# First tap of the gated recurrence's convolution on ScalarE; the WKV recurrence with its inverse's products unit by unit, a third buffer, and two output stores a half step

## The chip, the cores and the metric

The kernel runs on one core of one Trainium2 chip. The metric is device time in microseconds (us); the time before is the median of three runs. TensorE (PE), VectorE (DVE), ScalarE (ACT), GpSimd (POOL) and the queues that issue DMA transfers (here nearly all on SyncE, SP) run side by side, each in its own order. TensorE has two clocks, 1.2 and 2.4 GHz; the profile gives the granted share of the higher one.

## The reference, cut to what matters

One layer: a normed, modulated input `h` (1024 latent tokens and 256 context tokens, 1024 channels) goes through two token mixers, the merged result through a SwiGLU. The two recurrences:

```python
def directional_conv(u, w, bias, reverse):          # 4 taps per channel
    ...
    out = bias
    for j in range(LRU_CONV):
        off = LRU_CONV - 1 - j if reverse else j
        out = out + w[j] * up[:, off:off + L]
    return out
def wkv7_scan(r, w, k, v, a, b, S0):                # S: 16 heads of 64x64, two directions
    def step(S, inp):
        r_t, w_t, k_t, v_t, a_t, b_t = inp
        sa = jnp.einsum('dbhij,dbhj->dbhi', S, a_t)
        S = S * w_t[..., None, :] + sa[..., :, None] * b_t[..., None, :] + v_t[..., :, None] * k_t[..., None, :]
        y = jnp.einsum('dbhij,dbhj->dbhi', S, r_t)
        return S, y
```

The first recurrence (1280 channels, both directions) takes its gates from the convolved input and is a scan `h = a*h + b`. The second (WKV) is a matrix-valued scan over the tokens. After it, `y` of both directions is summed and group-normed per head.

## The kernel before

Float32 throughout; the dense products are split into a high and a low part and made in three matmuls (L88 to L90). By the trace the program has five stages: 95 to 760 us the in-projections with the first recurrence beside them; 760 to 1490 the operands of the WKV recurrence; 1490 to 2206 the WKV recurrence, with the last of its operands and of the 32x32 inverses beside its first steps, the output projection of the first recurrence (`pol`, L1107) and the group norms as fill; then the rest of the group norms and the merge; from 2345 the SwiGLU, in which TensorE is full. A scheduler puts each engine's instructions into an order from dependencies and priorities, so an edit in one place can move instructions of others.

**First recurrence** (`lru_tiles`). For each pair of 120-channel tiles, direction and stretch of tokens (512 wide, or 256 for the context), `conv` loads `lup` (L383), zeroes its edges on POOL (L380, L382), and makes `lxc` on VectorE: the first tap as a `tensor_scalar` with weight and bias (L386), three more taps on top (L388). Then `lh` and `ll` (L398, L399) feed the gate matmuls `pg` (L415), ScalarE makes the sigmoids and exponentials (L54), POOL two products (L430, L432), VectorE the scan. There are 66 tiles; `lxc` has four buffers and `lup` five. Each tile of the in-projection needs `whi` (VectorE, L230), `wlo` (POOL, L231), and an eviction of its result `pin` on ScalarE (L258, L296 and others).

**WKV recurrence** (`wkv_chain`). 32 tokens are one step; 40 steps, the first 8 the context's. The 16 heads of two directions are 32 units; each step has two half steps `a` = 0 and 1 of 16 units, in two chains that are woven together. The state and the step's other vectors sit in a tile `tvu` of 128 rows: 64 of state, 32 of `v` (loaded by L969 through `new_tvu`, one step ahead), 32 of `u`. A half step:

1. `ru`: 16 matmuls of 128 rows x 32 columns (out<-in `ru<-tvu,skb`), one a unit, four column groups in turn; copy to `rs` (helper L993, by turn on VectorE or ScalarE).
2. `rs` times the unit's inverse (`ru<-rs,xbd`): four matmuls of 128x128, each with a block-diagonal `xbd` of four 32x32 inverses. `xbd` is put together by four copies a step on VectorE (L1025, for both halves at once) from the loaded tile `xc`; POOL zeroed the rest once. Four copies (L993) take the result into `tvu[96:128]`.
3. `pn`: 16 matmuls of 128 rows x 64 columns make the next state, two copies (L993), or every second step products with the decay (L1063), put it into the other buffer of `tvu`.
4. `py`: 16 matmuls make the outputs (steps from 8 on), one copy to `ys`, and four stores (L1013) of 32x256 into `y_d[2, SEQ, D]`.

Group norms (L1246 to L1289) load 128 tokens of `v`, gate and both directions of `y`, one DMA each; six of the eight run within the recurrence.

The product with the inverses:

```python
for v in range(0 if UT else 4):
    mm(t[:, 1, v], xb[:, a * 4 + v].rearrange("p a b -> p (a b)"), r[:, v])
```

`t` (`ru`) is one PSUM bank of 2 KB a partition. `pm` (L676, an operand of the recurrence) is the only product now that uses tiles of fewer than 128 rows in its main stage: four 64x64 tiles in turn, and the two row halves write different banks.

Of the kernel before, what the change touches and what calls it, by code (L numbers as in the profile page):

```python
# [10 lines left out]
AF = mybir.ActivationFunctionType  # L11
ALU = mybir.AluOpType
# [17 lines left out]
NSTEP = T // 32  # L30
# [313 lines left out]
def lru_tiles(k, pool, ps):  # L344
# [6 lines left out]
    nc, act = k.nc, k.act  # L351
# [18 lines left out]
    def conv(p, d, q):  # L370
        o, w = LQ[q]
        base, end = (SEQ, T) if q == 0 else (0, SEQ)
        out = []
        for t in ts(p):
            r = slice(0, rows(t))
            up = tile_(f"lup{t}_{d}_{q}", "lup", (LT, 516))
            lo = o - 3 if d == 0 else o
            x, y = max(lo, base), min(lo + w + 3, end)
            if x > lo:
                nc.gpsimd.memset(up[r, 0:3], 0.0)  # L380
            if y < lo + w + 3:
                nc.gpsimd.memset(up[r, w:w + 3], 0.0)  # L382
            nc.sync.dma_start(up[r, x - lo:y - lo], k.ux_d[t * LT:t * LT + rows(t), x:y])  # L383
            xc = tile_(f"lxc{t}_{d}_{q}", "lxc")[r, 0:w]
            tap = lambda j: up[r, j:j + w] if d == 0 else up[r, 3 - j:3 - j + w]
            nc.vector.tensor_scalar(xc, tap(3), k.lcw[r, t, d, 3:4], k.lcb[r, t, d:d + 1], ALU.mult, ALU.add)  # L386
            for j in range(3):
                nc.vector.scalar_tensor_tensor(xc, tap(j), k.lcw[r, t, d, j:j + 1], xc, ALU.mult, ALU.add)  # L388
            out.append(xc)
        return out  # L390
# [69 lines left out]
    units = [(p, d, q) for p in range((NT + 1) // 2) for d in range(2) for q in LORD[d]]  # L460
    k.act_last = prev = None
    nxt = conv(*units[0])
    gws = None
    for n, u in enumerate(units):
        p, d, q = u
# [4 lines left out]
        cur = gates(*u, xcs, gws)  # L470
# [437 lines left out]
FILLA = 0  # L908
ROUNDS = ((0, 1), (2, 3), (4, 5), (6, 7), (8,), (9,))
FPTS = ((0, 0), (38, 1), (40, 1))  # L910
UT = 0
NEND = 3
SETV = 0
SETDVE = 0
XDVE = 40
XACT = 0
PACE = 1
MORE = (1, 2, 3)
NRD = 3
# [10 lines left out]
def wkv_setup(k):  # L930
    nc, bp = k.nc, k.bp
    z = lambda n, sh: bp.tile(sh, F32, name=n)
    k.ska = [z(f"ska{i}", [P, NU, 64]) for i in range(NRING)]
    k.skb = [z(f"skb{i}", [P, NU, 64]) for i in range(NRING)]
    for i, t in enumerate(k.ska):
        nc.scalar.copy(t[0:64], bcast(k.ident[0:64, 0:64], 1, NU))
    if not UT:
        k.xbd = [z(f"xbd{i}", [P, 8, 4, 32]) for i in range(2)]
        for t in k.xbd:
            (nc.vector if SETDVE & 2 else nc.gpsimd).memset(t, 0.0)  # L940
    k.tvu = [[z(f"tvu{a}_{i}", [P, 2, 8, 64]) for i in range(2)] for a in range(2)]
# [18 lines left out]
def chunk_id(s, d):  # L960
    b, c = chunk(s, d)
    return 4 * b + c


def new_tvu(k, s, a):
    nc = k.nc
    src = pair(k.v_d.rearrange("(c s) f -> c s f", s=32), chunk_id(s, 0), chunk_id(s, 1))
    t = k.tvu[a][s % 2]
    nc.sync.dma_start(t[64:96].rearrange("p d h i -> p d (h i)"), src[:, :, a * 512:a * 512 + 512].rearrange("d s f -> s d f"))  # L969
    return t  # L970

# [13 lines left out]
def wkv_chain(k, a):  # L985
# [3 lines left out]
    def mm(*a, **b):  # L989
        k.pe_last = nc.tensor.matmul(*a, **b, start=True, stop=True).ins.name  # L990
# [8 lines left out]
    def outputs(s, tvu):  # L999
        if s < 8:  # L1000
            return
        skb = k.skb[s % NRING]
        py = k.psb2.tile([P, 4, 64], F32, name=f"py{s}_{a}", tag="py", bufs=1)
        for v, g, gr, d, i in units:
            mm(py[gr, v], skb[:, unit(d, i), 0:32], tvu[:, d, i])
        ys = k.op.tile([P, 256], F32, name=f"ys{s}_{a}", tag="ys", bufs=4)
        copy(ys, py.rearrange("p v i -> p (v i)"))
        for d in range(2):
            r = 32 * chunk_id(s, d)
            for h in range(2):  # L1010
                g = 2 * d + h
                c = a * 512 + h * 256
                nc.sync.dma_start(k.y_d[d, r:r + 32, c:c + 256], ys[32 * g:32 * g + 32])  # L1013

    cur, nxt, prev = None, new_tvu(k, 0, a), None
    for t in k.tvu[a]:
        (nc.vector if a < SETV else nc.gpsimd).memset(t[96:P], 0.0)
    for s in range(NSTEP):
        ska, skb = k.ska[s % NRING], k.skb[s % NRING]
        if not UT:  # L1020
            xb = k.xbd[s % 2]
        if a == 0 and not UT:
            for g in range(4):
                gr = slice(32 * g, 32 * g + 32)
                (nc.scalar.copy if s < XACT else nc.vector.tensor_copy if s < XDVE else nc.gpsimd.tensor_copy)(xb[gr, :, g], k.xc[s // 4][gr, s % 4].rearrange("p a v t -> p (a v) t"))  # L1025
        prev, tvu = cur, nxt
        cur = tvu
        ahead = lambda: new_tvu(k, s + 1, a) if s + 1 < NSTEP else None
        if a == 1:
            nxt = ahead()  # L1030
        t = ps.tile([P, 2, 4, 64], F32, name=f"ru{s}_{a}", tag="ru", bufs=2)
        seen = slice(0 if s else 64, P)
        for v, g, gr, d, i in units:
# [4 lines left out]
        if a == 0:  # L1038
            if s > 0:
                outputs(s - 1, prev)  # L1040
            nxt = ahead()
            yield
        for v, g, gr, d, i in units if UT else ():
            mm(t[gr, 1, v], k.xc[s // 4][gr, s % 4, a, v], r[gr, v])
        for v in range(0 if UT else 4):
            mm(t[:, 1, v], xb[:, a * 4 + v].rearrange("p a b -> p (a b)"), r[:, v])
        for g in range(4):
            copy(tvu[96:P, g // 2, g % 2 * 4:g % 2 * 4 + 4], t[32 * g:32 * g + 32, 1])
        yield
# [184 lines left out]
def group_norm(k, pool, ps, tb, out=None):  # L1234
# [7 lines left out]
    flat = lambda t: t.rearrange("p a i -> p (a i)")  # L1242
    y, v, g = big("gy"), big("gv"), big("gg")
    y1 = k.c1p.tile([P, NH, 64], F32, name="gy1_7") if tb == 7 else big("gy1")
    for t, src in ((v, k.v_d), (g, k.gate_d), (y, k.y_d[0]), (y1, k.y_d[1])):
        nc.sync.dma_start(flat(t), src[tok])  # L1246
        for _ in range(GNY):
            yield
    yield
# [251 lines left out]
def scratch(k):  # L1501
    d = k.dpool
    t = lambda n, s: d.tile(s, F32, name=n)
    k.ux_d = t("ux_d", [LRU, T])
    k.lru_d = t("lru_d", [LRU, SEQ])
    k.uy_d = t("uy_d", [LRU, SEQ])
    k.gl_d = t("gl_d", [D, SEQ])
    k.gr_d = t("gr_d", [D, SEQ])
    k.gate_d = t("gate_d", [SEQ, D])
    k.rw_d = t("rw_d", [2, 2, P, KD, 512])  # L1510
    k.v_d = t("v_d", [T, D])
    k.skb_d = [t(f"skb{i}_d", [n, P, NU, 64]) for i, n in enumerate((NSTEP - 8, 8))]
# [183 lines left out]
```

## Time and profile before

| | |
|---|---|
| median of three runs | 3172.0 us (3169.22 to 3175.68) |
| profiled execution | 3170.86 us |
| its span | 3168.8 us |
| PE, DVE, ACT, POOL busy | 87%, 63%, 45%, 33% |
| mean granted PE clock | 0.904 |

The profile is one execution. Its page gives each engine's busy time, the span in 40 slices, the chain that ended last, and groups of instructions with the idle time ahead of them and what ended it; the trace behind it can be asked by stage, line, tile and stretch. "PEld" is the loading of weights into TensorE. A float32 matmul stands twice in the trace, so 16 matmuls are 32 records.

### The profile page before, as it was taken

How to read it: one execution, taken by the hardware profiler on the slowest of the kernel's cores; microseconds unless marked ns; L12 is line 12 of the kernel's file. 1: busy time of each engine (PE TensorE's matmuls, PEld its weight loads, DVE VectorE, ACT ScalarE, POOL GpSimd, SP SyncE). 2: the span in 40 equal slices, each digit the busy share in tenths (PEclk: the TensorE clock that was granted, in tenths of full speed). 3: DMA queues.
4: the chain of work that ended last, by engine and by line, in shares of the span. 5: the costliest groups of instructions: out<-in, count | busy, mean ns of one | idle time of the engine just before them, and what ended most of it. 6: DMA issues, size and time to landing. Idle time of an engine off the chain costs nothing. (4 is left out here: it accounts for less than half of the span.)

```text
span 3168.8 us, 53672 instructions
## 1 busy us (share of the span) xinstructions
PE 2772.7 (87%) x20606; PEld 2235.2 (71%) x20606; DVE 2010.8 (63%) x3067; ACT 1410.4 (45%) x2579; POOL 1037.3 (33%) x896
## 2 busy tenths in 40 slices
PE   5888888789898878887889878788899999999998
PEld 4767666667777666765666767566678888888888
DVE  7688989894667887878874434675686423232234
ACT  3465757474467555767333433344425111111114
POOL 4344435452445545666333220323441000000000
PEclk9999899999899878987558978788999999999999
DMA  5334333322455455555766777776772211111112
GB/s 201 105 107 128 115 109 118 111 76 74 142 145 143 114 123 128 131 140 136 192 189 213 220 210 206 222 240 220 266 284 85 98 57 54 37 57 40 46 57 71
DMA packets 374726, 428.96 MB, mean 135 GB/s; under 512 B 135446, under 2 KB 279238, under 8 KB 366534
## 3 DMA queue, kind: packets, MB, share of 16 engines
q1 hardware_dynamic: 374470, 425.53, 45.4%
q8 instruction: 163, 2.67, 0.4%
q14 instruction: 93, 0.76, 0.1%
HBM read 286.87 MB, written 126.26 MB: 130 GB/s over the span
## 5 line engine op out<-in xcount | busy, mean ns | idle before, releaser
L88 PE MATMUL pin<-h1024hi,whi 128*128 128x512 f32 (+1 forms) x1024 | 431.9, 422 | 47.0 <-DVE whi L230 15.2
L90 PE MATMUL pin<-h1024hi,wlo 128*128 128x512 f32 (+1 forms) x1024 | 425.8, 420 | 26.0 <-POOL wlo L231 16.8
L89 PE MATMUL pin<-h1024lo,whi 128*128 128x512 f32 (+1 forms) x1024 | 427.2, 417 | 4.1 <-DVE h1024lo L120 4.1
L231 POOL TENSOR_TENSOR wlo<-wraw,whi 128x512 fp32r<-128x512 f32 (+1 forms) x144 | 229.7, 1595 | 339.8 <-DVE whi L230 135.0
L88 PEld LDWEIGHTS pin<-h1024hi,whi 128*128 128x128 f32 (+1 forms) x1024 | 205.2, 201 | 100.8 <-DVE whi L230 21.3
L90 PEld LDWEIGHTS pin<-h1024hi,wlo 128*128 128x128 f32 (+1 forms) x1024 | 204.8, 200 | 80.6 <-POOL wlo L231 23.1
L89 PEld LDWEIGHTS pin<-h1024lo,whi 128*128 128x128 f32 (+1 forms) x1024 | 204.2, 199 | 51.3 <-DVE h1024lo L120 6.6
L54 ACT ACT_TABLE_LOAD x164 | 210.4, 1283 | 17.2 <-DVE gd L499 5.9
L990 PE MATMUL pn<-tvu,ska 128*64 128x64 f32 (+1 forms) x2496 | 159.8, 255 | 34.9 <-DVE tvu L993 20.1
L1444 DVE TENSOR_TENSOR sil<-sil,pfu 128x512 f32<-128x512 f32 x44 | 30.2, 687 | 243.2 <-PE pfu L90 243.2
L990 PEld LDWEIGHTS pn<-tvu,ska 128*64 128x64 f32 (+1 forms) x2496 | 122.8, 161 | 75.9 <-DVE tvu L993 23.3
L388 DVE SCALAR_TENSOR_TENSOR lxc<-lup,c_lru_conv_w,lxc 120x512 f32<-120x512 f32 (+3 forms) x198 | 159.4, 835 | 0.4
L1452 DVE SCALAR_TENSOR_TENSOR x<-pfo,modv,x 128x512 f32<-128x512 f32 (+1 forms) x112 | 74.2, 670 | 132.4 <-PE pfo L90 132.4
L990 PE MATMUL ru<-tvu,skb 128*32 128x64 f32 (+1 forms) x2560 | 107.7, 260 | 49.9 <-ACT tvu L993 26.0
L993 ACT COPY tvu<-ru 32x256 f32<-32x256 f32 x193 | 69.9, 362 | 151.8 <-DVE tvu L993 99.4
L68 ACT CAST whi_fi<-wraw_fi 128x1024 fp32r<-128x1024 f32 x48 | 50.6, 1053 | 168.3 <-PE pfg L89 53.0
L990 PE MATMUL ru<-rs,xbd 128*128 128x64 f32 x640 | 113.3, 335 | 12.4 <-ACT rs L993 8.3
L415 PE MATMUL pg<-lh,gw 120*120 120x512 f32 (+3 forms) x264 | 95.4, 373 | 32.4 <-DVE lh L398 29.7
L990 PEld LDWEIGHTS ru<-tvu,skb 128*32 128x32 f32 (+1 forms) x2560 | 69.5, 131 | 75.9 <-ACT tvu L993 28.5
L680 ACT COPY bc<-pm 32x256 f32<-32x256 f32 x160 | 98.5, 616 | 52.6 <-PE pm L676 50.3
L721 DVE TENSOR_TENSOR X<-X,it 128x62 f32<-128x62 f32 (+25 forms) x186 | 119.1, 640 | 3.9
L720 DVE TENSOR_TENSOR it<-bp,X 128x62 f32<-128x62 f32 (+25 forms) x186 | 118.3, 636 | 3.8
(374 smaller groups left out, 7660.8 us busy)
## 6 DMA issues: line engine op xcount, KB each, us to landing
skb<-skb_d SPq DMA_DIRECT2D x40, 1024.0 KB
wraw<-in_w_in_dram SPq DMA_DIRECT2D x142, 256.0 KB
wraw_fi<-in_w_ffn_in_dram SPq DMA_DIRECT2D x48, 512.0 KB
skb_d<-kr SPq DMA_DIRECT2D x160, 128.0 KB
ska_d<-km SPq DMA_DIRECT2D x160, 128.0 KB
skb_d<-km SPq DMA_DIRECT2D x160, 128.0 KB
ska<-ska_d SPq DMA_DIRECT2D x40, 512.0 KB
wmr<-in_w_modT_dram SPq DMA_DIRECT2D x32, 512.0 KB
```

Source lines behind the costliest of these rows:

```text
L54: ins = self.nc.scalar.activation(*a, **b).ins
L88: nc.tensor.matmul(out, wh, xh, start=first, stop=False)
L89: nc.tensor.matmul(out, wh, xl, start=False, stop=False)
L90: nc.tensor.matmul(out, wl, xh, start=False, stop=last)
L231: (nc.gpsimd if INLO else nc.vector).tensor_tensor(lo, raw, hi.bitcast(F32), ALU.subtract)
L388: nc.vector.scalar_tensor_tensor(xc, tap(j), k.lcw[r, t, d, j:j + 1], xc, ALU.mult, ALU.add)
L415: nc.tensor.matmul(pg[r, g, 0:w], gw[r, v, g * LT:g * LT + rows(t)], m, start=(x == 0), stop=(x == len(passes) - 1))
L680: nc.scalar.copy(bc[g, :, 4 * i:4 * i + 4].rearrange("s t e h -> s h e t"), pm[64 * c + 32:64 * c + 64, :, d, :, 32:64])
L720: nc.vector.tensor_tensor(tv, bpt[:, :, t + 1:32, t:t + 1].to_broadcast(sh), X[:, :, t:t + 1, 0:t + 1].to_broadcast(sh), ALU.mult)
L721: nc.vector.tensor_tensor(X[:, :, t + 1:32, 0:t + 1], X[:, :, t + 1:32, 0:t + 1], tv, ALU.add)
L990: k.pe_last = nc.tensor.matmul(*a, **b, start=True, stop=True).ins.name
L1452: nc.vector.scalar_tensor_tensor(x, p[:, 0:n], k.modv[:, 40 + o, 0:1], x, ALU.mult, ALU.add)
```

## The change

Four edits:

1. The first tap (L386) is a ScalarE activation (Identity, with weight and bias as pointers) in place of the VectorE `tensor_scalar`.
2. `xbd`, its 160 copies and its two memsets are gone. The product with the inverses is made by 16 matmuls of 32x32 tiles, read directly from `xc`: unit by unit, row group and column group moving together.
3. `tvu` has three buffers, and `v` is loaded two steps ahead.
4. `y_d` is laid out so that a half step's outputs are stored by two transfers of 64x256; the group norm loads each direction of `y` in four pieces of 32 rows.

In numbers, over the program: 320 matmuls `ru<-rs,xbd` become 1280 `ru<-rs,xc`; VectorE loses 160 copies and 66 taps; ScalarE gains 66 activations, with as many table loads as before; SP loses 256 stores of 32x256 and 16 loads of `y`, and gains 128 stores of 64x256 and 64 loads of `y`.

```diff
-            nc.vector.tensor_scalar(xc, tap(3), k.lcw[r, t, d, 3:4], k.lcb[r, t, d:d + 1], ALU.mult, ALU.add)
+            nc.scalar.activation(xc, tap(3), AF.Identity, bias=k.lcb[r, t, d:d + 1], scale=k.lcw[r, t, d, 3:4])
...
-    if not UT:
-        k.xbd = [z(f"xbd{i}", [P, 8, 4, 32]) for i in range(2)]
-        for t in k.xbd:
-            (nc.vector if SETDVE & 2 else nc.gpsimd).memset(t, 0.0)
-    k.tvu = [[z(f"tvu{a}_{i}", [P, 2, 8, 64]) for i in range(2)] for a in range(2)]
+    k.tvu = [[z(f"tvu{a}_{i}", [P, 2, 8, 64]) for i in range(3)] for a in range(2)]
...
-    t = k.tvu[a][s % 2]
+    t = k.tvu[a][s % 3]
...
-            r = 32 * chunk_id(s, d)
-            for h in range(2):
-                g = 2 * d + h
-                c = a * 512 + h * 256
-                nc.sync.dma_start(k.y_d[d, r:r + 32, c:c + 256], ys[32 * g:32 * g + 32])
+            nc.sync.dma_start(k.y_d[d, chunk_id(s, d), 2 * a:2 * a + 2].rearrange("h t f -> (h t) f"), ys[64 * d:64 * d + 64])
...
-        if a == 0 and not UT:
-            for g in range(4):
-                gr = slice(32 * g, 32 * g + 32)
-                (nc.scalar.copy if s < XACT else nc.vector.tensor_copy if s < XDVE else nc.gpsimd.tensor_copy)(xb[gr, :, g], k.xc[s // 4][gr, s % 4].rearrange("p a v t -> p (a v) t"))
...
-        ahead = lambda: new_tvu(k, s + 1, a) if s + 1 < NSTEP else None
+        cur, nxt = tvu, nn
+        ahead = lambda: new_tvu(k, s + 2, a) if s + 2 < NSTEP else None
...
-        for v, g, gr, d, i in units if UT else ():
+        for v, g, gr, d, i in units:
             mm(t[gr, 1, v], k.xc[s // 4][gr, s % 4, a, v], r[gr, v])
-        for v in range(0 if UT else 4):
-            mm(t[:, 1, v], xb[:, a * 4 + v].rearrange("p a b -> p (a b)"), r[:, v])
...
+            for c in range(4):
+                nc.sync.dma_start(flat(t)[32 * c:32 * c + 32].rearrange("t (b f) -> t b f", f=256),
+                                  k.y_d[src, 4 * tb + c].rearrange("b t f -> t b f"))
...
-    k.y_d = t("y_d", [2, SEQ, D])
+    k.y_d = t("y_d", [2, SEQ // 32, 4, 32, 256])
```

**TensorE in the first steps of the WKV recurrence.** Before, where step 1's product with the inverses stands (`pm` is an operand's product of a later stretch; the digit behind `ru`, `rs`, `pn` is the half):

```order
L990 MATMUL ru_0_15090<-tvu_1_14854,skb_14844 32x64 x4
L676 MATMUL pm_0_14213<-kr_0_1_14198,kb_0_1_14197 64x64 x15
L990 MATMUL ru_0_15090<-rs_0_15107,xbd_14850 128x64 x4
L990 MATMUL ru_1_15149<-tvu_1_14856,skb_14844 32x64 x16
L676 MATMUL pm_0_14213<-kr_0_1_14198,kb_0_1_14197 64x64
```

After, the same step's second half:

```order
L982 MATMUL pn_0_15198<-tvu_1_14850,ska_14841 64x64 x4
L982 MATMUL ru_1_15179<-rs_1_15196,xc_14860 32x64 x5
L982 MATMUL pn_0_15198<-tvu_1_14850,ska_14841 64x64
L982 MATMUL ru_1_15179<-rs_1_15196,xc_14860 32x64
L982 MATMUL pn_0_15198<-tvu_1_14850,ska_14841 64x64
L982 MATMUL ru_1_15179<-rs_1_15196,xc_14860 32x64
```

The four products that stood together are sixteen, and eleven of them stand one at a time between single `pn` of the other half. Before, such a run of single matmuls stands there too, of `ru` and `pn`, ahead of the rows shown. Counted over the order from the first `ru` to the first `py`, TensorE changes the shape of its tile 228 times before and 331 times after; from the first to the last `py` 366 and 429 times.

**TensorE in a latent step.** Before (`pol` is the fill):

```order
L990 MATMUL py_0_17972<-tvu_1_14854,skb_14844 32x64 x5
L990 MATMUL ru_0_17953<-tvu_0_14853,skb_14845 32x64 x16
L990 MATMUL ru_1_17899<-rs_1_17916,xbd_14850 128x64 x4
L1107 MATMUL pol_0_17714<-llo_3_17640,olh_0_17705 128x512
L1107 MATMUL pol_0_17714<-lhi_3_17639,oll_0_17706 128x512
```

After:

```order
L982 MATMUL pn_1_17190<-tvu_1_14853,ska_14841 64x64 x16
L982 MATMUL py_1_17233<-tvu_1_14853,skb_14844 32x64 x4
L982 MATMUL ru_0_17149<-rs_0_17166,xc_16554 32x64 x16
L1087 MATMUL pol_6_16804<-lhi_6_14979,oll_6_16796 128x512
L1087 MATMUL pol_6_16804<-lhi_7_14989,olh_6_16795 128x512
```

The sixteen stand together here; the fill behind them has another tile shape than they, where `xbd` and the fill had the same.

**VectorE in an odd latent step.** Before:

```order
L993 COPY rs_1_18552<-ru_1_18535 128x256
L993 COPY rs_0_18606<-ru_0_18589 128x256
L1025 COPY xbd_14850<-xc_18375 32x8x32 x4
L993 COPY tvu_1_14856<-ru_1_18535 32x256
L993 COPY tvu_0_14853<-ru_0_18589 32x256 x2
L1063 TENSOR_TENSOR tvu_0_14855<-pn_1_18632,pb 64x512 x2
```

After, in such a step:

```order
L985 COPY rs_1_19318<-ru_1_19301 128x256
L1043 TENSOR_TENSOR tvu_2_14851<-pn_0_19320,pb 64x512 x2
L985 COPY tvu_1_14853<-ru_1_19301 32x256
L985 COPY rs_0_19381<-ru_0_19364 128x256
L1043 TENSOR_TENSOR tvu_2_14854<-pn_1_19405,pb 64x512 x2
```

The four copies into `xbd` are gone from between the chain's own copies; the rest is turned over a little.

**ScalarE in the first recurrence.** Before:

```order
L54 ACTIVATE lg_0_2_2403<-lg_0_2_2403,cpos 120x512
L54 ACT_TABLE_LOAD
L54 ACTIVATE lg_1_0_2476<-pg_1_0_2467,c_lru_ba 120x256
L54 ACTIVATE lg_1_0_2478<-pg_1_0_2467,c_lru_bx 120x256
L493 ACTIVATE zv_4169<-held_4172,cmu 128x512
```

After:

```order
L54 ACTIVATE lg_0_2_2403<-lg_0_2_2403,cpos 120x512
L386 ACTIVATE lxc_1_2_2442<-lup_1_2_2439,c_lru_conv_b,c_lru_conv_w 120x512
L54 ACT_TABLE_LOAD
L54 ACTIVATE lg_1_0_2476<-pg_1_0_2467,c_lru_ba 120x256
L54 ACTIVATE lg_1_0_2478<-pg_1_0_2467,c_lru_bx 120x256
L296 COPY ev_0_4267<-pin_0_4205 128x512
L386 ACTIVATE lxc_1_2_2450<-lup_1_2_2447,c_lru_conv_b,c_lru_conv_w 120x512
```

The taps stand between the sigmoids of the gates (`lg<-pg`) and the evictions of the in-projection (`ev<-pin`).

## Rows read from the trace of the kernel before

**Rows 1.** Busy time of each engine (instructions), clock, DMA share, GB/s, by stage.
```profile
95.00:760.00 665.00, 567.20 (x2588) 449.06 (x2587) 542.24 (x808) 403.29 (x609) 300.85 (x250) 0.95 0.36 111
...
1490.00:1700.00 210.00, 168.92 (x1581) 127.28 (x1580) 163.12 (x290) 79.88 (x163) 75.09 (x75) 0.57 0.71 196
1700.00:2206.00 506.00, 418.05 (x7089) 335.60 (x7087) 255.39 (x443) 195.06 (x461) 138.50 (x76) 0.83 0.72 217
...
2345.00:3168.00 823.00, 814.32 (x3732) 680.53 (x3730) 310.93 (x445) 196.79 (x312) 28.70 (x12) 1.00 0.20 66
```

**Rows 2.** What TensorE waited for between 95 and 760 us: total, times, longest.
```profile
PE pg L415 <- DVE lh L398: 29.7, 13, 5.2
PE pin L90 <- POOL wlo L231: 11.4, 5, 4.5
...
PE pin L88 <- ACT ux L258: 7.1, 2, 4.1
```

**Rows 3.** VectorE by line, 95 to 760 us: busy, mean ns, idle before.
```profile
L388 DVE SCALAR_TENSOR_TENSOR lxc<-lup,c_lru_conv_w,lxc 120x512 f32<-120x512 f32 (+3 forms) x198 | 159.4, 835 | 0.4
...
L386 DVE TENSOR_SCALAR lxc<-lup,c_lru_conv_w,c_lru_conv_b 120x512 f32<-120x512 f32 (+3 forms) x66 | 46.6, 715 | 8.0 <-DMA lup<-ux_d 7.6
```

**Rows 4.** ScalarE by line, 95 to 760 us.
```profile
L296 ACT COPY ev<-pin 128x512 f32<-128x512 f32 x30 | 17.4, 582 | 46.3 <-PE pin L90 35.6 <-DVE zv L499 10.7
...
L493 ACT ACTIVATE zv<-held,cmu 128x512 f32<-128x512 f32 x16 | 11.5, 717 | 0.2
```

**Rows 5.** What engines waited for between 1490 and 2206 us.
```profile
ACT tvu L993 <- DVE tvu L993: 118.5, 70, 6.3
...
PE ru L990 <- DMA tvu<-v_d: 5.4, 4, 2.1
```

**Rows 6.** Weight loads on TensorE in time, full clock: start, us, records.
```profile
1906.52 0.97 PEld L990 LDWEIGHTS ru<-rs,xbd 128*128 128x128 f32 x8
...
1908.38 0.52 PEld L990 LDWEIGHTS ru<-tvu,skb 128*32 128x32 f32 x32
1908.99 0.19 PEld L990 LDWEIGHTS pn<-tvu,ska 128*64 128x64 f32 x2
```

**Rows 7.** The same at half clock, in the first steps.
```profile
1530.42 0.18 PEld L990 LDWEIGHTS ru<-tvu,skb 128*32 128x32 f32 x2
1530.77 0.29 PEld L990 LDWEIGHTS pn<-tvu,ska 64*64 64x64 f32 x2 [0.17 <-issue]
1531.17 0.18 PEld L990 LDWEIGHTS ru<-tvu,skb 128*32 128x32 f32 x2
...
1538.33 0.94 PEld L676 LDWEIGHTS pm<-kr,kb 64*64 64x64 f32 x30 [0.17 <-issue]
1539.38 1.78 PEld L990 LDWEIGHTS ru<-rs,xbd 128*128 128x128 f32 x8
1541.28 0.84 PEld L990 LDWEIGHTS ru<-tvu,skb 128*32 128x32 f32 x32
```

**Rows 8.** VectorE's copies into `xbd`, 1490 to 1700 and 1700 to 2206 us.
```profile
L1025 DVE COPY xbd<-xc 32x256 f32<-32x256 f32 x37 | 13.7, 370 | 2.1 <-PE ru L990 1.6
...
L1025 DVE COPY xbd<-xc 32x256 f32<-32x256 f32 x124 | 53.5, 432 | 31.1 <-PE ru L990 28.2
```

**Rows 9.** VectorE in time in an odd latent step, and near a group norm.
```profile
1936.85 1.23 DVE L1025 COPY xbd<-xc 32x256 f32<-32x256 f32 x4 [0.60 <-PE ru L990]
1938.11 0.42 DVE L993 COPY tvu<-ru 32x256 f32<-32x256 f32 x1
...
2051.99 5.24 DVE L1025 COPY xbd<-xc 32x256 f32<-32x256 f32 x4
```

**Rows 10.** The output stores on SP's queue in time, and group norm loads of `y`.
```profile
1958.47 2.57 SPq L1013 DMA_DIRECT2D y_d<-ys  x4
1961.08 1.03 SPq L969 DMA_DIRECT2D tvu<-v_d  x1
...
L1246 SPq DMA_DIRECT2D gy<-y_d x15: 319/346/588, 2002.4 to 2220.0; - x15
```

More of the change, by code (lines that the diff above doesn't have):

```diff
@@ L910 @@
 FPTS = ((0, 0), (38, 1), (40, 1))
-UT = 0
 NEND = 3
 SETV = 0
-SETDVE = 0
-XDVE = 40
-XACT = 0
 PACE = 1
@@ L1008, in outputs @@
         for d in range(2):
-            r = 32 * chunk_id(s, d)
-            for h in range(2):
-                g = 2 * d + h
-                c = a * 512 + h * 256
-                nc.sync.dma_start(k.y_d[d, r:r + 32, c:c + 256], ys[32 * g:32 * g + 32])
-    cur, nxt, prev = None, new_tvu(k, 0, a), None
+            nc.sync.dma_start(k.y_d[d, chunk_id(s, d), 2 * a:2 * a + 2].rearrange("h t f -> (h t) f"), ys[64 * d:64 * d + 64])
+    cur, nxt, nn, prev = None, new_tvu(k, 0, a), new_tvu(k, 1, a), None
     for t in k.tvu[a]:
@@ L1019, in wkv_chain @@
         ska, skb = k.ska[s % NRING], k.skb[s % NRING]
-        if not UT:
-            xb = k.xbd[s % 2]
-        if a == 0 and not UT:
-            for g in range(4):
-                gr = slice(32 * g, 32 * g + 32)
-                (nc.scalar.copy if s < XACT else nc.vector.tensor_copy if s < XDVE else nc.gpsimd.tensor_copy)(xb[gr, :, g], k.xc[s // 4][gr, s % 4].rearrange("p a v t -> p (a v) t"))
         prev, tvu = cur, nxt
-        cur = tvu
-        ahead = lambda: new_tvu(k, s + 1, a) if s + 1 < NSTEP else None
+        cur, nxt = tvu, nn
+        ahead = lambda: new_tvu(k, s + 2, a) if s + 2 < NSTEP else None
         if a == 1:
-            nxt = ahead()
+            nn = ahead()
         t = ps.tile([P, 2, 4, 64], F32, name=f"ru{s}_{a}", tag="ru", bufs=2)
@@ L1040, in wkv_chain @@
                 outputs(s - 1, prev)
-            nxt = ahead()
+            nn = ahead()
             yield
-        for v, g, gr, d, i in units if UT else ():
+        for v, g, gr, d, i in units:
             mm(t[gr, 1, v], k.xc[s // 4][gr, s % 4, a, v], r[gr, v])
-        for v in range(0 if UT else 4):
-            mm(t[:, 1, v], xb[:, a * 4 + v].rearrange("p a b -> p (a b)"), r[:, v])
         for g in range(4):
@@ L1244, in group_norm @@
     y1 = k.c1p.tile([P, NH, 64], F32, name="gy1_7") if tb == 7 else big("gy1")
-    for t, src in ((v, k.v_d), (g, k.gate_d), (y, k.y_d[0]), (y1, k.y_d[1])):
-        nc.sync.dma_start(flat(t), src[tok])
+    for t, src in ((v, k.v_d), (g, k.gate_d), (y, 0), (y1, 1)):
+        if t is v or t is g:
+            nc.sync.dma_start(flat(t), src[tok])
+        else:
+            for c in range(4):
+                nc.sync.dma_start(flat(t)[32 * c:32 * c + 32].rearrange("t (b f) -> t b f", f=256),
+                                  k.y_d[src, 4 * tb + c].rearrange("b t f -> t b f"))
         for _ in range(GNY):
```

## The prediction, made before the changed kernel had run

> **What bounds the kernel now.** I read the stage table first [rows 1]. From 2345 us on TensorE is busy 814 of 823 us at full clock; nothing of the change is there. In the stretch of the first recurrence (95 to 760) TensorE is busy 567 of 665 us and VectorE 542, so the two share the bound; the reader sees in [rows 2] that the largest single wait of TensorE there is for VectorE's `lh`, 29.7 us, and that ScalarE's evictions cost it 7.1. In the WKV recurrence (1490 to 2206) no engine is full. In its first 210 us the clock is 0.57 with TensorE busy 169 and VectorE 163; from 1700 on TensorE is busy 418 of 506 us at a clock of 0.83, VectorE 255, ScalarE 195. What sets the pace there is the round of the two chains, PE to copy to PE, as ScalarE's 118.5 us of waits for VectorE's `tvu` copies show [rows 5]. DMA moves 217 GB/s at a share of 0.72 [rows 1]: not the bound, but near enough to take back a part of any gain.
>
> The sum is made against the profiled execution, 3170.9 us (span 3168.8 and 2.1 around it), which is 1.1 us under the median 3172.0.
>
> **First tap to ScalarE.** VectorE loses 66 taps of 715 ns, 46.6 us [rows 3]. ScalarE pays for each about what its nearest row costs, an Identity with pointers, 128x512 in 717 ns [rows 4]: at most 66 x 0.717 = 47 us, on an engine busy 403 of 665 us; two thirds of the tiles have that width, the rest are shorter, so some 42. The work therefore moves at its price. What it is worth is the share of TensorE's wait for `lh` that falls. The three other taps stay on VectorE (159.4 us) and must now wait for ScalarE, behind sigmoids and evictions; and an eviction queued behind a tap that waits for its load or for a free `lxc` holds up TensorE's next `pin`. Bounds: -25 us (nearly all of the 29.7) and +15 (twice the 7.1 that evictions cost now). I take a quarter of the 29.7: **-8**.
>
> **The product with the inverses, first steps (1490 to 1700).** Before, eight records of 128x128 take 1.78 us at half clock [rows 7] and 0.97 at full [rows 6]. No row shows a 32x32 tile. Its two neighbours: `ru`, which also takes four column groups in turn, makes 32 records in 0.84 us at half clock [rows 7] and 0.52 at full [rows 6]; `pm`, which takes two row halves and two column halves, makes 30 in 0.94 at half clock [rows 7]. So tiles that differ in rows do overlap, at least when they write different banks. I take `ru`: 0.94 us less per half step at half clock, 0.45 at full. At a clock of 0.57 (one seventh of the time at full) that is 0.87 x 16 half steps = 14 us of TensorE less.
>
> Against it stand the tile shapes: 103 more changes of shape in this stretch. Their price is in the alternation of single `ru` and `pn` at half clock: the pair comes back every 0.75 us (1530.42 to 1531.17) [rows 7], and its four records need some 0.1 to 0.15 of that (0.84/32 and 0.94/30 us each, in the groups of the same rows), so a change costs about 0.31 us; 103 of them 32 us. The Trainium skill has the same ("TensorEngine Tiling (Array Packing)", Key Properties): changing the tiling mode, and not just the tile, drains the TensorE. The trace agrees, with its 0.31 us, and the rule speaks against this change. Net, 32 - 14 = +18 on an engine that is idle a fifth of this stretch; half on the path: +9. VectorE loses 13.7 us of copies [rows 8] in a stretch where it is busy 163 of 210 us; half counts: -7. Together **+2** (bounds -17 and +25).
>
> **The same in the latent steps (1700 to 2206).** At a clock of 0.83, two thirds at full, a half step saves 0.67 x 0.45 + 0.33 x 0.94 = 0.61 us, times 64 = 39 us of TensorE. There are 63 more changes of shape, since `pol` behind the product no longer has its shape. At full clock the price lies between 0.09 us (the gap from the end of the last `ru` load to the first `pn`, 1908.90 to 1908.99 [rows 6]) and the 0.31 above; 0.25 x 63 = 16. Net -23; TensorE is busy 0.83 of the time and each chain waits for the other, so 0.6 of it counts: **-14** (bounds -39 and +5).
>
> VectorE loses 124 copies, 53.5 us [rows 8]. They stand in the chain: at 1936.85 a block of 1.23 us, and 0.03 us behind it the `tvu` copy that ScalarE and then TensorE wait for; beside a group norm, when POOL also works, a block took 5.24 us [rows 9]. The group's mean is 432 ns against 0.31 in the undisturbed block, so some 15 of the 53.5 us are stretching. Not all is on the path, since a copy behind often waits for TensorE anyway: I take half, **-27** (bounds -53 and 0).
>
> **Stores, third buffer, loads of `y`.** Four stores held SP's queue 2.57 us, and the load of the next `v` stood right behind them [rows 10]; two stores are half of that. What that cost TensorE is 5.4 us of waits for `tvu` from DMA [rows 5], and a load two steps ahead takes most: **-4**. A block's group norm issues six more loads at 0.346 us [rows 10], 2 us on SP, and reads pieces of 1 KB; that may start the norm's VectorE work later: **+3** (0 to +10).
>
> **What DMA takes back.** The latent steps would shrink by about 45 of 506 us with the same bytes; the share goes from 0.72 to 0.79. Nothing is full on average, but the loads of a step would be late oftener: a quarter of the 45, **+11**.
>
> Sum: -8 + 2 - 14 - 27 - 4 + 3 + 11 = -37; 3170.9 - 37 = 3133.9, with the 1.1 to the median **3135 us**.
>
> **Rivals.**
>
> A. *Row groups in one bank do not overlap* (slower). `pm` writes its two row halves into different banks; in the change all four row groups write one bank, `ru`. If there each tile waited for the one ahead, a record would take four times that of `ru`: 4 x 0.52 = 2.1 us at full clock instead of 0.97, 4 x 0.84 = 3.4 at half instead of 1.78. With two thirds of the time at full clock that is 0.67 x 1.1 + 0.33 x 1.6 = 1.28 us more per latent half step, x 64 = 82 us, and with the 16 of the shapes 0.6 x 98 = +59 on the path where the forecast has -14; in the first steps 1.5 x 16 = 24, with the 32 of the shapes half of 56, +28 where it has +9. With no shrinking the +11 of DMA falls away: 3135 + 73 + 19 - 11 = 3216. If only every second record waited, half of that is added, 3175; I put A at 3200. It decides as soon as the group takes over about 1.3 us at full clock. For it: nothing in the trace shows four row groups in one bank. Against: `pm` shows that rows as such are no obstacle, and neighbours write different partitions. Beside this, the Trainium skill has it as a rule ("TensorEngine Tiling (Array Packing)", Restrictions and Gotchas): different row tiles cannot access the same PSUM bank at the same time. By that rule the time is A's, without it the forecast's; no run here shows it yet.
>
> B. *No change.* The alternating order of the first steps falls wholly on the path (+18 instead of +9), VectorE's copies prove to be covered except for the stretching (-15 instead of -27), and the taps cost ScalarE's evictions what they give VectorE (0 instead of -8): -37 + 9 + 12 + 8 = -8, with less for DMA to take back some -5 to +5: about 3170. For it: VectorE's rows show many waits beside the blocks. Against: the 0.03 us behind the block [rows 9].
>
> C. *More.* Taps -20, VectorE's copies -45, DMA takes back nothing: -37 - 12 - 18 - 11 = -78, 3094. For it: the clock, 0.83 and 0.57, would rise if TensorE's gaps close; against: the DMA share.
>
> **How the numbers follow.** Forecast 0.50 (3105 to 3160), A 0.18, B 0.20, C 0.12. About 0.2%, 6 us, is what a measurement of this kernel can tell from no change. Faster: 0.48 of the forecast, 0.12 of C, 0.04 of B, 0.64; same: 0.02 and 0.07 of B, 0.09; slower: 0.18 of A and 0.09 of B, 0.27. The likeliest's own range is 3105 to 3160; for 8 in 10 it reaches a little past C's and A's values: 3088 to 3205.
>
> **What would show it.** In the changed kernel's trace the group `ru<-rs,xc` should take 0.5 to 0.6 us for 32 records at full clock (A: 2 us); no copy of over 0.5 us should stand between chain copies on VectorE in latent steps, and these steps should take 1.2 us less on the mean; in the first steps single `ru<-rs,xc` and `pn` should alternate at 0.75 us a pair; TensorE's wait for `lh` should fall from 29.7 to about 20 with a wait for ScalarE of under 15 beside it. The prediction is wrong if the stretch 1490 to 2206 shrinks by less than 10 us or the one before it grows.

## The result

| | us, median | runs | ratio to the kernel before (95%) |
|---|---|---|---|
| before, beside it | 3170.61 | 4 | |
| changed kernel | 3124.64 | 4 | 0.9847 (0.9832 to 0.9861) |

The changed kernel is 46 us faster. The prediction was 3135, 37 us under the 3172.0 it started from, in a range of 3088 to 3205. Its profiled span is 3123.3 us. The table splits the two profiled executions at matmuls that both have (start to start, in us).

| stretch | before | after | difference |
|---|---|---|---|
| start to the first `pm` (first recurrence) | 860.2 | 843.1 | -17.0 |
| first `pm` to the first `ru` of step 12 (operands, first steps) | 902.5 | 917.3 | +14.8 |
| step 12 to the last `py` (latent steps) | 431.1 | 383.1 | -47.9 |
| last `py` to the first `pfg` | 226.7 | 231.3 | +4.6 |
| first `pfg` to the end | 748.5 | 748.5 | 0.0 |

Step 12 is the cut, not step 8 as in the prediction, because the fill moves across step 8: of the 480 `pol` matmuls 90 stand ahead of it before and 44 after, but 182 stand ahead of step 12 in both.

By stage (columns as in [rows 1]), after, the first steps and the latent steps:

```profile
1486.00:1760.00 274.00, 236.57 (x3027) 167.42 (x3026) 150.50 (x275) 92.40 (x190) 88.09 (x79) 0.68 0.70 196
1760.00:2144.00 384.00, 296.05 (x7462) 224.61 (x7463) 169.84 (x274) 169.65 (x409) 105.03 (x59) 0.90 0.82 236
```

The same stretches of the kernel before:

```profile
1502.00:1763.00 261.00, 225.12 (x2479) 171.33 (x2482) 175.91 (x323) 92.18 (x192) 87.02 (x78) 0.67 0.71 202
1763.00:2194.00 431.00, 345.66 (x6106) 278.42 (x6095) 225.94 (x384) 170.50 (x411) 108.32 (x60) 0.81 0.71 213
```

In the latent steps TensorE is busy 50 us less, its clock is 0.90 instead of 0.81, and DMA moves 236 GB/s instead of 213. In the first steps TensorE is busy 11 us more although VectorE is busy 25 less.

TensorE's waits in the first recurrence, after (answers to [rows 2]):

```profile
PE pg L415 <- DVE ll L399: 14.2, 12, 3.2
PE pin L88 <- ACT ux L258: 10.6, 4, 4.5
PE pin L88 <- ACT held L509: 9.9, 5, 4.8
PE pg L415 <- DVE lh L398: 8.8, 14, 1.3
PE pin L90 <- POOL wlo L231: 6.0, 6, 1.3
```

Three rows of the same list before:

```profile
PE pin L90 <- POOL lup L380: 9.0, 1, 9.0
...
PE pg L415 <- DVE ll L399: 6.0, 8, 1.7
...
PE pin L88 <- ACT held L509: 1.2, 1, 1.2
```

The wait for `lh` fell from 29.7 to 8.8 us, but the one for `ll`, made from the same `lxc` right behind it, rose from 6.0 to 14.2: VectorE's two together fell by 12.7 us. The waits for ScalarE's evictions (`ux` and `held`) rose by 12.2 and took that back. What is left are TensorE's waits for POOL: 11.4 us for `wlo` and one of 9.0 before, 6.0 us after. The one of 9.0 us stands behind a single `wlo` split that took POOL 10.0 us, where the median of the 66 is 1.6; VectorE runs taps and splits back to back beside it. The tap on ScalarE itself, and what it waited for and who for it:

```profile
L386 ACT ACTIVATE lxc<-lup,c_lru_conv_b,c_lru_conv_w x66: 584/808/835, 112.0 to 671.8; 120x512 f32<-120x512 f32 x40, 120x256 f32<-120x256 f32 x20, 80x512 f32<-80x512 f32 x4, 80x256 f32<-80x256 f32 x2
...
  DVE lg L434: 59.7, 32
...
  DVE lxc L388: 16.2, 10
```

Its median is 808 ns, not the 717 of the row it was priced by [rows 4]. ScalarE stood idle 59.7 us ahead of taps, until VectorE's L434 had freed one of the four `lxc`.

The product with the inverses, weight loads on TensorE after, at full and at half clock (answers to [rows 6] and [rows 7]):

```profile
1922.83 0.49 PEld L982 LDWEIGHTS ru<-rs,xc 32*32 32x32 f32 x32
1923.41 0.19 PEld L1087 LDWEIGHTS pol<-llo,olh 128*128 128x128 f32 x1
...
1932.58 0.84 PEld L982 LDWEIGHTS ru<-rs,xc 32*32 32x32 f32 x32 [0.17 <-issue]
1933.59 0.29 PEld L1087 LDWEIGHTS pol<-lhi,olh 128*128 128x128 f32 x1 [0.17 <-issue]
```

32 records take 0.49 us at full clock and 0.84 at half, as `ru<-tvu,skb` did (0.52 and 0.84). In the first steps they alternate with `pn`, at 0.75 us a pair (matmuls, after):

```profile
1530.35 0.42 PE L982 MATMUL ru<-rs,xc 32*32 32x64 f32 x2
1530.69 0.47 PE L982 MATMUL pn<-tvu,ska 128*64 128x64 f32 x2
1531.10 0.42 PE L982 MATMUL ru<-rs,xc 32*32 32x64 f32 x2
```

### The profile page after: what moved, and what is told of

Read it like the earlier page. It is cut to its first block, busy times and chain, and to the rows that moved or that the text cites. A ratio compares the mean times of both kernels' runs of the same rounds, so it can differ in the third digit from the quotient of the medians.

```text
span 3123.3 us, 57216 instructions
## 1 busy us (share of the span) xinstructions
PE 2730.1 (87%) x22526; PEld 2168.8 (69%) x22526; DVE 1904.5 (61%) x2841; ACT 1454.4 (47%) x2645; POOL 1011.7 (32%) x896
## 5 line engine op out<-in xcount | busy, mean ns | idle before, releaser
L90 PE MATMUL pin<-h1024hi,wlo 128*128 128x512 f32 (+1 forms) x1024 | 424.4, 418 | 11.8 <-POOL wlo L231 11.4
L231 POOL TENSOR_TENSOR wlo<-wraw,whi 128x512 fp32r<-128x512 f32 (+1 forms) x144 | 212.8, 1478 | 309.9 <-DVE whi L230 153.7
L230 DVE CAST whi<-wraw 128x512 fp32r<-128x512 f32 (+1 forms) x144 | 77.5, 539 | 66.0 <-PE pin L89 27.7
L982 PE MATMUL ru<-tvu,skb 128*32 128x64 f32 (+1 forms) x2560 | 96.0, 242 | 21.2 <-DVE tvu L985 8.4
L982 PE MATMUL ru<-rs,xc 32*32 32x64 f32 x2560 | 87.1, 243 | 30.8 <-issue 15.7
L432 POOL TENSOR_TENSOR lxc<-la 120x512 f32<-120x512 f32 (+3 forms) x66 | 84.9, 1288 | 79.8 <-ACT la L54 68.0
```

The source lines that it names most:

```text
L90: nc.tensor.matmul(out, wl, xh, start=False, stop=last)
L230: nc.vector.tensor_copy(hi, raw)
L231: (nc.gpsimd if INLO else nc.vector).tensor_tensor(lo, raw, hi.bitcast(F32), ALU.subtract)
L432: nc.gpsimd.tensor_tensor(xc, a, a, ALU.mult)
```

## The experiments

Twelve kernels ran, in three sets; each set has its own runs of the kernel before beside it, on one chip. Single runs of a kernel spread by up to 23 us in these sets, and a profiled execution can lie 11 us under its kernel's median; so totals are read from the ratios and stages from the traces, and a stage is believed to some 10 us: with the tap alone, which edits nothing behind the first recurrence, the stretch from the first `pm` to step 12 took 911.5 us (902.5 before) and the latent steps 421.0 (431.1).

| kernel | us, median | ratio to before (95%) |
|---|---|---|
| tap alone | 3155.85 | 0.9948 (0.9927 to 0.9968) |
| units alone | 3140.82 | 0.9902 (0.9883 to 0.9922) |
| tap and stores | 3138.32 | 0.9905 (0.9888 to 0.9921) |
| change again | 3125.96 | 0.9855 (0.9831 to 0.9879) |
| change, tap undone | 3137.38 | 0.9885 (0.9862 to 0.9909) |
| change, stores undone | 3151.56 | 0.9932 (0.9910 to 0.9953) |
| change, third buffer undone | 3103.11 | 0.9779 (0.9756 to 0.9803) |
| change, third buffer, load of `v` late | 3126.79 | 0.9863 (0.9846 to 0.9879) |
| change, copies added (free) | 3138.16 | 0.9882 (0.9860 to 0.9905) |
| change, copies added (pinned) | 3141.06 | 0.9902 (0.9885 to 0.9919) |
| change, groups held | 3115.54 | 0.9824 (0.9799 to 0.9848) |
| two buffers, groups held | 3109.19 | 0.9798 (0.9778 to 0.9818) |

### The parts one by one

**The change again**, unaltered (no edit).

> The changed kernel once more, unaltered, so that the three others stand beside it on one chip. Every theory: a ratio to the kernel before of 0.985, as in the first result, some 46 us.

Measured 0.9855; the first result, 0.9847, lies within its interval.

**The tap alone**, on the kernel before.

```diff
-            nc.vector.tensor_scalar(xc, tap(3), k.lcw[r, t, d, 3:4], k.lcb[r, t, d:d + 1], ALU.mult, ALU.add)
+            nc.scalar.activation(xc, tap(3), AF.Identity, bias=k.lcb[r, t, d:d + 1], scale=k.lcw[r, t, d, 3:4])
```

> The kernel before with the first tap on ScalarE and nothing else. Theory 'parts' (each edit has its own worth, read from its own stage): the first recurrence's stretch shrinks by about 16 us, as in the changed kernel (first matmul of the WKV operands 860.2 to 843.1 us), all else stays: 3150 to 3160 us. Rival 'order' (the scheduler turns over the whole program with every edit, and the worth of a part is mostly that of the new order): 3164 to 3177 us, with the first stretch shorter but later ones longer.

Measured 0.9948, some 16 us. The first `pm` starts at 844.5 us instead of 860.2.

**The tap undone** in the changed kernel.

```diff
-            nc.scalar.activation(xc, tap(3), AF.Identity, bias=k.lcb[r, t, d:d + 1], scale=k.lcw[r, t, d, 3:4])
+            nc.vector.tensor_scalar(xc, tap(3), k.lcw[r, t, d, 3:4], k.lcb[r, t, d:d + 1], ALU.mult, ALU.add)
```

> The changed kernel with the first tap back on VectorE. 'Parts': 13 to 20 us longer, 3138 to 3145 us, and TensorE's wait for lh in the first recurrence back near 30 us. 'Order': within 6 us of the changed kernel, 3119 to 3131 us.

Measured 0.9885 against 0.9855, some 10 us with overlapping intervals; the first `pm` at 859.2, and the wait is back:

```profile
PE pg L415 <- DVE lh L398: 29.8, 13, 5.7
...
PE pin L90 <- POOL lup L380: 9.0, 1, 9.0
```

The single wait of 9.0 us for POOL is back too. So the tap is worth 10 to 16 us, in the stage where it stands.

**The units alone**: a switch of the kernel before selects them, and the copies and `xbd` go with it.

```diff
-UT = 0
+UT = 1
```

> The kernel before with the product with the inverses unit by unit (no block-diagonal tile, no copies into it) and nothing else; two buffers, four stores, tap on VectorE. 'Parts': the first steps lengthen by about 10 us as in the changed kernel, the latent steps shrink by 35 to 48: 3135 to 3148 us. 'Order': 3160 to 3177 us. A rival within 'parts', that the third buffer and the stores bring the latent steps' gain: no shorter than 3155 us.

Measured 0.9902, 31 us, as 'parts' had it; latent steps 410.6 us against 431.1. The first steps did not lengthen, against that theory: 899.6 us from the first `pm` to step 12, 902.5 before. But a wait of TensorE grew in them:

```profile
PE ru L990 <- DMA tvu<-v_d: 15.0, 8, 4.9
```

It was 5.4 us [rows 5]. With the shorter product TensorE comes to wait for the load of `v`, which spoke for the third buffer. So the buffer was taken away alone.

### The third buffer

**Two buffers**, `v` loaded one step ahead; all else as changed.

```diff
-    k.tvu = [[z(f"tvu{a}_{i}", [P, 2, 8, 64]) for i in range(3)] for a in range(2)]
+    k.tvu = [[z(f"tvu{a}_{i}", [P, 2, 8, 64]) for i in range(2)] for a in range(2)]
...
-        ahead = lambda: new_tvu(k, s + 2, a) if s + 2 < NSTEP else None
+        ahead = lambda: new_tvu(k, s + 1, a) if s + 1 < NSTEP else None
```

> The changed kernel with two buffers of tvu and v loaded one step ahead again. The prediction's term for buffer and stores together was 4 us: 0 to 5 us longer than the changed kernel. Theory 'load' (with units alone, TensorE's wait for tvu from DMA rose from 5.4 to 15.0 us in the latent steps, so the shorter product made the load of v late): 10 to 25 us longer, with that wait back at 10 to 15 us.

Neither: 0.9779 against 0.9855, 23 us *shorter*. The third buffer costs time. With two buffers and two stores the wait for `v` is nearly gone as well:

```profile
PE ru L982 <- DMA tvu<-v_d: 0.2, 1, 0.2
```

From the first `pm` to step 12 the two-buffer kernel takes 899.6 us (changed kernel 917.3, and 909.9 when run again), in the latent steps 376.8 (383.1 and 388.2). Its first and latent steps:

```profile
1466.00:1742.00 276.00, 219.36 (x3126) 159.41 (x3126) 166.11 (x297) 104.34 (x218) 95.12 (x89) 0.73 0.70 198
1742.00:2119.00 377.00, 302.33 (x7490) 228.91 (x7489) 175.58 (x276) 170.82 (x412) 107.72 (x60) 0.88 0.84 244
```

**Three buffers, load late**: which half of the edit is it?

```diff
-    t = k.tvu[a][s % 2]
+    t = k.tvu[a][s % 3]
```

(on the two-buffer kernel, with the third buffer allocated).

> The changed kernel with three buffers but v loaded one step ahead, as before. If the third buffer loses by the order it allows TensorE in the first steps (331 changes of shape against 262 with two): as slow as the changed kernel, 3120 to 3131 us. If it loses by the early load: as fast as with two buffers, 3098 to 3108 us.

Measured 0.9863: as slow as the changed kernel. It is the buffer, not the early load. The scheduler's order has 331 changes of tile shape from the first `ru` to the first `py` with three buffers, whichever way `v` is loaded, and 262 with two. But this kernel loses elsewhere than the changed one: from the first `pm` to step 12 it takes 908.3 us, in the latent steps 397.8, 21 us more than with two buffers.

**Groups held**: in the first 8 steps each group of 16 matmuls of either chain is ordered behind the one ahead of it (an order on TensorE alone, no semaphore).

```diff
+    def group(s):
+        k.grp = k.pe_last if s < GRP else None
+
     def mm(*a, **b):
-        k.pe_last = nc.tensor.matmul(*a, **b, start=True, stop=True).ins.name
+        ins = nc.tensor.matmul(*a, **b, start=True, stop=True).ins
+        if k.grp is not None:
+            k.tc.add_manual_dep(ins, k.grp, NOSYNC, reason="pace")
+        k.pe_last = ins.name
...
```

(`group(s)` stands ahead of `ru`, the product and `pn`; `GRP = 8`.)

> The changed kernel with the order of TensorE held in the first 8 steps: each group of 16 matmuls of the two chains follows the one ahead of it whole, so that no single matmuls alternate; changes of tile shape from the first ru to the first py fall from 331 to 117. By the prediction's price of 0.31 us a change at half clock, 66 us of TensorE go; if half is on the path, as predicted for the added ones, 20 to 33 us shorter, 3092 to 3105 us. Rival, that VectorE's inverses set the first steps' pace: within 6 us of the changed kernel, though the shape changes are gone. Third, that the held order makes one chain wait for the other: 5 to 15 us longer.

Measured 0.9824 against 0.9855, some 10 us (intervals overlap), between the first theory and the second. Stages of this kernel, to be held against the changed kernel's above:

```profile
1489.00:1739.00 250.00, 167.77 (x3009) 128.01 (x3012) 147.40 (x273) 90.48 (x188) 85.19 (x77) 0.73 0.76 213
1739.00:2136.00 397.00, 303.71 (x7494) 230.23 (x7490) 172.74 (x280) 169.87 (x413) 110.20 (x62) 0.86 0.81 231
```

TensorE is busy 69 us less in the first steps, 167.8 against 236.6, nearly the 66 that 0.31 us a change gave. (The clock is 0.73 instead of 0.68 there, so the whole 69 is not the shapes' alone.) A third of it shortens that stretch, 274 to 250; the latent steps, which were not touched, are longer in this trace (397 against 384 and 388), and part of the gain is gone by the end.

**Two buffers and groups held**, the two edits together.

> The changed kernel with two buffers and with TensorE's groups of the first 8 steps held together; changes of tile shape from the first ru to the first py 126, against 262 with two buffers alone and 331 in the changed kernel. If the loss by the third buffer is the alternation that it lets in, the two overlap: 3090 to 3103 us. If they are separate things (23 and 10 us): 3090 to 3095. If the held order delays the operands: over 3103.

Measured 0.9798 against 0.9779 of two buffers alone: no gain, and 3109.19 us lies where a held order that delays the operands had put it (over 3103), though the intervals overlap. The 136 changes of shape fewer take TensorE's busy time in the first steps from 219.4 to 189.0 us, yet the stretch stays (276 and 274 us). With two buffers the alternation that is left costs nothing that holding it back regains. That the third buffer costs 23 us is shown. That it costs them by the changes of shape is not: the 9 to 18 us that the three-buffer kernels lose between the first `pm` and step 12 fit it, but that is hardly more than a stage varies by, and holding the groups and taking the buffer away both move the fill as well (4 `pol` ahead of step 8 in place of 44). Why the latent steps are 6 to 21 us longer with three buffers is open.

### The stores

**Stores undone** in the changed kernel: four stores a half step, one load of `y` per direction.

```diff
-            nc.sync.dma_start(k.y_d[d, chunk_id(s, d), 2 * a:2 * a + 2].rearrange("h t f -> (h t) f"), ys[64 * d:64 * d + 64])
+            r = 32 * chunk_id(s, d)
+            for h in range(2):
+                g = 2 * d + h
+                c = a * 512 + h * 256
+                nc.sync.dma_start(k.y_d[d, r:r + 32, c:c + 256], ys[32 * g:32 * g + 32])
```

> The changed kernel with four stores a half step and one load of y per direction in the group norm again. The prediction: about 0, between 5 us shorter (six loads of y fewer per group norm) and 5 us longer (SP's queue held 2.6 us in place of 1.3 by the stores of a half step). Rival, that SP's queue bounds the latent steps once the product is shorter: 10 to 20 us longer.

Measured 0.9932 against 0.9855: 26 us longer, beyond the 10 to 20 of the rival, and far from the prediction's 5. Latent steps 406.2 us against 388.2 in the same set.

**Tap and stores** on the kernel before (with the layout of `y_d` and the loads of `y`); it differs from the two-buffer kernel only by the product with the inverses.

```diff
-            nc.vector.tensor_scalar(xc, tap(3), ...
+            nc.scalar.activation(xc, tap(3), ...
...
-                nc.sync.dma_start(k.y_d[d, r:r + 32, c:c + 256], ys[32 * g:32 * g + 32])
+            nc.sync.dma_start(k.y_d[d, chunk_id(s, d), 2 * a:2 * a + 2].rearrange("h t f -> (h t) f"), ys[64 * d:64 * d + 64])
```

> The kernel before with the tap on ScalarE and the two stores a half step (with the layout and loads of y that go with them); block-diagonal product and two buffers stay. Against the changed kernel with two buffers, the only difference is the product with the inverses. If the parts add (tap 17 us, stores 26 as when they were undone): 3127 to 3135 us, and the units' product would be worth 25 to 30. If the stores pay only once the product is short, 3150 to 3157 us, and the two together would be worth some 50.

Measured 0.9905, between the two: with the tap's 16 us off, the stores are worth some 14 without the units and 26 with them. The units on top of tap and stores bring 0.9905 to 0.9779, 40 us; of these the two traces place 5 before step 12, 13 in the latent steps and 9 behind them.

How the stores do it was looked for on SP's queue. What SP waited for in the latent steps, tap alone:

```profile
SPq L1013 <- DMA skb<-skb_d: 56.6, 20, 4.1
SPq L982 <- PE pn L990: 16.1, 9, 5.0
...
SPq L1013 <- DMA ska<-ska_d: 14.4, 10, 2.7
...
SPq L1246 <- DMA y_d<-ys: 6.9, 3, 4.3
```

and with two stores a half step:

```profile
SPq L982 <- PE pn L990: 32.3, 10, 10.3
SPq L1246 <- DMA y_d<-ys: 30.7, 9, 4.9
SPq L1009 <- DMA skb<-skb_d: 16.5, 6, 3.4
...
SPq L1009 <- DMA ska<-ska_d: 7.7, 7, 1.7
```

L1013 and L1009 are the stores, L1246 the group norm's loads. The queue stood 71.0 us in front of a store until some earlier load had landed, and 24.2 with half as many stores. But it then stood longer in front of other entries, for `pn` and for the stores that the group norm's loads read, and all its waits together are 209.7 us and 208.6. What fell is the time that it spends on issuing: 112 us for 226 stores to 66 for 113, and 200 to 178 us over all its transfers, the added loads of `y` included. The stage rows of the two (tap alone, then with the stores):

```profile
1756.00:2177.00 421.00, 340.37 (x6129) 274.85 (x6117) 222.93 (x385) 170.71 (x412) 108.25 (x60) 0.82 0.73 217
```

```profile
1748.00:2138.00 390.00, 322.50 (x6117) 261.53 (x6120) 215.18 (x377) 164.02 (x392) 100.43 (x58) 0.86 0.81 230
```

Nearly the same bytes (91 and 90 MB) go in less time, so DMA's share goes up from 0.73 to 0.81; TensorE runs at a higher clock and is busy less. (This second profile is 10 us under its kernel's median, so the 31 us between the rows overstate the stores.) Which late load then holds the chains was not isolated: no wait of TensorE, VectorE or ScalarE for a DMA falls by 20 us. ScalarE's wait for `olg`, behind which its `tvu` copies queue, is 26.6 us with four stores and 18.8 with two. The edit also changes the layout of `y_d` and cuts the loads of `y` into pieces, and neither was tried apart; so the worth of the edit is shown, and the way it works is not.

### VectorE's copies or TensorE's product

**Copies added, free**: four VectorE copies a step from `xc` into a tile that nobody reads.

```diff
+        if a == 0:
+            for g in range(4):
+                gr = slice(32 * g, 32 * g + 32)
+                nc.vector.tensor_copy(k.scr[gr], k.xc[s // 4][gr, s % 4].rearrange("p a v t -> p (a v) t"))
```

> The changed kernel with VectorE's four copies a step added again, into a tile that nobody reads; TensorE's product stays unit by unit. It does extra work whose result is unused. If the gain of the latent steps is VectorE's (the copies stood between the chain's own): 20 to 35 us longer, 3145 to 3160 us. If it is TensorE's (0.65 us for the product in place of 1.10 at full clock): no more than 8 us longer, up to 3133 us.

Measured 0.9882 against 0.9855, some 9 us with overlapping intervals: between the two theories. Since nothing held these copies in place, they went to other places than before. So they were tied down.

**Copies added, pinned**: the same four, from `rs` of the first half.

```diff
         copy(r, t[:, 0])
+        if a == 0:
+            for g in range(4):
+                gr = slice(32 * g, 32 * g + 32)
+                nc.vector.tensor_copy(k.scr[gr], r[gr].rearrange("p v i -> p (v i)"))
```

> The changed kernel with four VectorE copies of 32x256 a step, from rs of the first half into a tile that nobody reads, so that they stand where the block-diagonal copies stood (behind rs, between the chain's copies). Extra work whose result is unused. If the units' gain is VectorE's, as the prediction had it for 27 of its 41 us: 20 to 35 us longer than the changed kernel, 3146 to 3160 us. If it is TensorE's: no more than 10 us longer, up to 3136 us.

Measured 0.9902 against 0.9855, 15 us, between the two again. Its stages:

```profile
1492.00:1779.00 287.00, 227.27 (x3055) 164.16 (x3058) 174.05 (x321) 91.38 (x190) 85.96 (x78) 0.70 0.66 185
1779.00:2161.00 382.00, 297.01 (x7449) 225.92 (x7438) 214.13 (x386) 166.38 (x404) 104.57 (x60) 0.89 0.83 239
```

In the latent steps VectorE is busy 44 us more than in the changed kernel, and they take 382 us against 384 and 388: nothing. The first steps take 287 against 274 and 273. The copies there, and in the latent steps:

```profile
L1023 DVE COPY scr<-rs 32x256 f32<-32x256 f32 x48 | 27.5, 573 | 1.6 <-ACT rs L986 0.8
...
L1023 DVE COPY scr<-rs 32x256 f32<-32x256 f32 x112 | 41.9, 374 | 15.0 <-ACT rs L986 12.0
```

So the pinned copies cost where VectorE has the inverses to make as well, and not in the latent steps, where they stand in gaps between the chain's own. Two limits: in the first steps the 48 pinned copies took 27.5 us, where 47 of the old ones into `xbd` had taken 15.9, and in the trace of the free copies the first steps take 270 us, no longer than without any. And nobody reads these copies; in the kernel before TensorE's product read `xbd`, and the copies into it waited for TensorE (28.2 us [rows 8]). That tie was not rebuilt, though no wait of TensorE for those copies stands in the trace of before.

## Why the prediction was right or wrong

The sign, the size and the range hold, but as a sum of terms of which several (VectorE's copies, the stores, the third buffer, what DMA takes back) were wrong by 10 to 27 us, in opposite directions. That the sum came out within 10 us is in good part luck.

- **Tap, -8.** Right in sign, small in size: 10 to 16 us; the way was right in part. I took a quarter of the wait for `lh`. VectorE's waits fell by 12.7 us (21 less for `lh`, 8 more for `ll`), and the waits for ScalarE's evictions that I feared took back 12.2 (20.5 us now, over the 15 that were to be a sign). The largest gain that is left in TensorE's waits is 14.4 us of waits for POOL, which I had not looked at; 9.0 of them are one wait, gone in the kernels with the tap on ScalarE and back when it was undone. The bound held. The price of a tap, 717 ns, was under the 808 measured.
- **The product, latent steps, -14.** The price is right, 0.49 us for the group as taken from `ru`, and the term fits: the units are worth 13 us of latent steps on top of tap and stores (376.8 against 390.0), 20 on the kernel before (410.6 against 431.1). Both include the removed copies, and neither is far outside what a stage varies by.
- **VectorE's copies, -27 in the latent steps.** Not borne out. Pinned copies cost nothing there. The step that failed is reading the 0.03 us between a block and the next chain copy [rows 9] as a delay of the chain: it shows that VectorE was not idle, not that the chain had nothing else to wait for. The same row group's waits of 28 us ahead of those copies [rows 8] said that VectorE had time. Yet the unit products with the copies gone are worth 31 us alone and 40 on top of tap and stores, as much as the 39 forecast for them (+2, -14, -27), while the stages account for 27 to 28: how the rest comes about is open, and a part for the copies that TensorE read is not excluded.
- **First steps, +2.** The price of a change of shape held (69 us of TensorE gone for 214 changes fewer, 0.32 each; 0.22 each with two buffers). Here VectorE's copies may count, -7 in the prediction, some 13 by the pinned copies and nothing by the free ones. The half that I put on the path was a third with three buffers and nothing with two. With two buffers the balance is about -3 against the kernel before (899.6 against 902.5 from the first `pm` to step 12), with the third +7 to +15, at the edge of what a stage can tell.
- **Stores and third buffer, -4.** Wrong twice. The stores are worth 14 to 26 us: I priced them by TensorE's wait for `tvu` (5.4 us [rows 5]), one consumer, when the queue serves all loads; half of the 2.57 us that four stores held SP [rows 10] is some 80 us of queue over the latent half steps (46 us measured, 22 with the added loads of `y`). The third buffer costs 23: I took more room as free of cost, although the order of the scheduler stood there with its 331 changes of shape, which I put down to the unit products; 69 of the 103 added ones go with the buffer.
- **What DMA takes back, +11.** Not seen: its share rose from 0.71 to 0.82, since much the same bytes went in 383 us instead of 431, and the latent steps shrank by the 48 us that the other terms had given (45). A share of 0.72 was read as a resource near its end; that the issuing queue is the limit instead is argued from the stores' worth, not shown.
- **Group norms, +3.** The stretch behind the last `py` grew by 4.6 us, less than a stage varies by.
- **Rivals.** A fell at once: four row groups that write one bank do overlap. The Trainium skill ("TensorEngine Tiling (Array Packing)", Restrictions and Gotchas) has it that different row tiles cannot access the same PSUM bank at the same time; here, where each writes its own 32 partitions, 32 records take 0.49 us, and the measurement decides. The Trainium skill's rule on modes ("TensorEngine Tiling (Array Packing)", Key Properties), that changing the mode drains TensorE, agrees with the 0.75 us a pair, now measured for 32x32 tiles too. B's mechanism, the alternation, is real: TensorE pays its price in the first steps. How much of that reaches the time with three buffers is not settled, and the stores' gain stood against it.

A version with all edits but the third buffer, 3103.11 us, beats both kernels: 0.9779 (0.9756 to 0.9803).

## What to carry to other kernels

Price a DMA removed by the time that its queue spends on issuing, not by one consumer's wait, and add up all waits of the queue: one that goes may come back in front of the next entry. Do the same with an engine's waits: the one for `lh` fell and the next one grew. A third buffer also gives a scheduler freedom; count what the new order does to tile shapes on TensorE, and try the buffer apart from the edit that seems to need it. That an engine runs two instructions back to back does not say that the second was late; look for idle time ahead of the first.

## What was not expected of the hardware

- Sixteen 32x32 products in four row and four column groups, all into one PSUM bank, load in 0.49 us at full clock and 0.84 at half, as fast as sixteen of 128x32 in four column groups.
- The 66 Identity activations with pointers for scale and bias took 808 ns at the median, 40 of them 120x512 and 20 half as wide, where one with a scale pointer alone took 717 on 128x512 [rows 4]. The 91 ns between them fit what the Trainium skill states ("ScalarE: Activation LUTs", What ACT_TABLE_LOAD costs): each such pointer operand adds about 93 ns. The prediction took a row with one pointer for an operation with two.
- SP's queue stood 71.0 us of 421 in front of stores until earlier loads had landed, and 24.2 of 390 with half as many stores of twice the size; yet all its waits together stayed as they were, 209.7 us and 208.6.
